# 24 of 50 input-projection tiles as 12 pairs of seven block products each

## Chip, cores and metric

The kernel runs on one core of a Trainium2 chip. The metric is the device time of one execution in microseconds (us); the profile shows one execution of it on that core. Engines are named as in the profile: PE is TensorE, DVE VectorE, ACT ScalarE, POOL GpSimd, SP the SyncE queue.

## What is computed

One layer of a decoder trunk for 2048 prompt tokens and 32 sample tokens (2080 columns in all). One input projection feeds attention (A), an S5 state-space branch with a gated linear unit (B) and a gated linear recurrence (C); each is multiplied by its SiLU gate, projected, merged with sigmoid gates, projected once more and normalized. All in float32.

```python
proj = x @ p['w_in']                                  # 1024 -> 6400 columns
q, k, v, g_a, u_b, g_b, x_c, g_c, g_m = jnp.split(proj, _split_points(), axis=-1)
attn = _attn_prompt(q, k, v, rel_bias, p['sinks'])    # or _attn_sample
y_b, h_re, h_im = _s5_branch(u_b, ...)
y_c, lru_h, conv_new = _rglru_branch(x_c, ...)
ya = (attn * jax.nn.silu(g_a)) @ p['w_br_a']          # yb, yc in the same way
merged = ga * ya + gb * yb + gc * yc                  # ga, gb, gc = sigmoid(g_m)
y = _layernorm(DN_ALPHA * x + merged @ p['w_out'], p['ln_g'], p['ln_b'])
```

## The kernel before

The 6400 projection columns are 50 tiles of 128: u (4 tiles, S5 input), x (4, recurrence input), k, v, q (4), m (24, merge gates), and gc, gb, ga (4 each, the branch gates). A tile is multiplied with five token units `UN` of 512, 512, 512, 272 and 272 columns. `gemm(i, u)` makes one unit: eight steps over the 1024 inputs, each three matmuls (`mm3`, L98 to L101) because every float32 operand is split into a high and a low part: high x high, high x low, low x high. Results lie in a ring of three PSUM banks `mm` and are evacuated by `evac`: u, x, k, v, q and m through `spill` (L187) to DRAM, m after a tanh; a gate tile is multiplied by its branch's result at once (tanh on ACT, two products on DVE, L104 and L229/L233), which `gate_load` has fetched from hD, zD or aD, and is stored to actD by SP (L1403).

Weights of a tile are loaded by SP (`w_load`, L163) into the one buffer `wr` and split into `wh` (ACT) and `wl` (DVE, L94).

The order is written by hand: the instructions of each engine stand in the order in which the program issues them. Between the matmuls of the tiles the program issues side work: `tick` adds up matmul time, and when the pace (`STEP` 4.6, or what a stream asks for) is reached, `side_step` takes the next step of the stream in front: `s5_stream`, then `glu_stream`, `lru_stream`, `attn_stream` and the sample part. The S5 head stores a table `biD` and reads it back as `bsD` (L308, L311), loads its C and D weights (L444, L448) and builds products for which TensorE's first matmul is at L466. The GLU makes two products for each of eight steps, into banks `sa` and `sb`, with `gelu_b` of the next step behind the second (names zs, zy, zh, zl). The recurrence makes 20 products L887 into `sa`, whose results four tanh read (names R, ig), then xf, the convolution of a later chunk and the split f. Attention has 32 steps, two for each of 16 blocks: scores in `sa`, S on DVE, probabilities split into pth and ptl, masks on GpSimd (L1082), products into `sb` (L1100).

After the tiles come the branch products (`py`, L99 to L101, from actD), which begin with the work of `seam`, and the output projection with the normalization (`po`, L1492 to L1494).

Of the kernel before, what the change touches and what calls it, by code (L numbers as in the profile page):

```python
# [16 lines left out]
T = 2080  # L17
# [13 lines left out]
GLU_WEIGHTS = 2.0  # L31
ATT_SCORE, ATT_SOFTMAX = 2.5, 3.5
# [4 lines left out]
         + [("m", i) for i in range(24)]  # L37
         + [("gc", i) for i in range(4)] + [("gb", i) for i in range(4)] + [("ga", i) for i in range(4)])
# [15 lines left out]
def kernel(ctx: ExitStack, tc: tile.TileContext, I, O):  # L54
# [28 lines left out]
    nD = dt_("nD", [2, 32, 128])  # L83
    bsD_t = dt_("bsD", [32, 132])
    bsD = bsD_t[:]
    actD = {b: dt_("actD" + b, [4, 128, T]) for b in "cba"}

# [45 lines left out]
    for u, (t0, n) in enumerate(UN):  # L133
        X[u] = (xhp.tile([128, 8, n], FR, name=f"xh{u}", tag=f"xh{u}"), xlp.tile([128, 8, n], FR, name=f"xl{u}"))
# [25 lines left out]
    def w_load(i):  # L160
        if i < len(TILES):
# [3 lines left out]
    def w_split(i):  # L165
        if i < len(TILES):
            wh = wpool.tile([128, 8, 128], FR, name=uid("wh"), tag="wh")
            wl = wpool.tile([128, 8, 128], FR, name=uid("wl"), tag="wl")
            split(wh, wl, WR.pop(i))
            WS[i] = (wh, wl)  # L170

    def gemm(i, u):
# [4 lines left out]
        for k in range(8):  # L177
            mm3(ps[:, :n], wh[:, k, :], wl[:, k, :], xh[:, k, :], xl[:, k, :], k == 0, k == 7)
            if k < 7:
                tick(n)  # L180
# [11 lines left out]
    def evac(kind, i, u, ps):  # L192
# [21 lines left out]
        elif kind == "m":  # L214
            spill(ps, n, mD[i][:, t0:t0 + n], AF.Tanh, 0.5)
        else:
            b = kind[1]
            gt = gp[0].tile([128, 512], FT, name=uid("gt"), tag="gt", bufs=2)[:, :n]
            br = gate_br.pop((b, i, u))
            act(gt, ps[:, :n], AF.Tanh, scale=0.5)  # L220
            stt(gt, gt, 1.0, ps[:, :n], OP.add, OP.mult)
            st = stage.tile([128, 512], FT, name=uid("st"), tag="st")[:, :n]
            if b == "b":
                nch = min(n, TP - t0) // 8
                V.tensor_mul(st[:, :nch * 8].rearrange("p (c j) -> p c j", j=8),
                             gt[:, :nch * 8].rearrange("p (c j) -> p c j", j=8),
                             br[:, :, 0:nch].rearrange("p j c -> p c j"))
                if u == 4:
                    V.tensor_mul(st[:, 240:272].rearrange("p (b t) -> p b t", t=4),  # L229
                                 gt[:, 240:272].rearrange("p (b t) -> p b t", t=4),  # L230
# [526 lines left out]
    def lru_stream():  # L757
# [123 lines left out]
        for i in range(4):  # L881
# [40 lines left out]
            if i + 1 < 4:  # L922
                yield
# [744 lines left out]
```

## Time and profile before

| | us |
|---|---|
| median of 3 runs | 1797.2 (1795.53 to 1797.56) |
| profiled execution | 1798.88 |
| its span, first to last instruction | 1797.1 |
| PE busy | 1775.0 (99%) |
| DVE busy | 1130.8 (63%) |
| ACT busy | 653.8 (36%) |
| POOL busy | 167.9 (9%) |

PE's busy share is that of the records, whose matmuls overlap a little; the step from one matmul to the next is read from the starts in the timeline. In brackets behind a row of the timeline stands how long the engine was idle before it, and what released it. A row of the waits lists engine and line, what it waited for, the total in us, how many times, and the longest.

### The profile page before, as it was taken

To read this page: it belongs to the slowest core of one execution; us is meant where nothing else is said; L and a number is where in the kernel's file an instruction comes from. 1 tells how busy PE (TensorE), PEld (TensorE's weight loads), DVE (VectorE), ACT (ScalarE), POOL (GpSimd) and SP (SyncE) were. 2 spreads that over 40 slices of the span, in tenths; PEclk is the share of its full clock that TensorE was granted. 3 is DMA by queue.
4 is the path that set the end of the run, shared out by engine and by line. 5 is a ranking of instruction groups with operands and counts; after the bars stand their busy time and mean duration, and the time that the engine had idled before them with its cause. 6 is when DMAs were issued, how large, how long until landed. Compare 5 with 4: busy or idle time off the path is not lost. (4 is left out here: it accounts for less than half of the span.)

```text
span 1797.1 us, 26615 instructions
## 1 busy us (share of the span) xinstructions
PE 1775.0 (99%) x9788; PEld 1549.5 (86%) x9788; DVE 1130.8 (63%) x2450; ACT 653.8 (36%) x1382; POOL 167.9 (9%) x377
## 2 busy tenths in 40 slices
PE   8999999999999999999999999999999999999998
PEld 7888888888899888888988888888888888888886
DVE  5755888886334456653777899654343557666666
ACT  6312443343333287674565655311220202111110
POOL 0000000000000000000355555400000000000000
PEclk9999999999999999999999999999999999999999
DMA  7443333433333334443332334453455646542222
GB/s 235 111 135 100 111 109 112 116 108 92 120 120 114 101 93 123 104 103 95 103 104 85 119 120 134 106 165 101 143 176 155 185 137 189 186 140 94 94 94 77
DMA packets 214038, 220.36 MB, mean 123 GB/s; under 512 B 89125, under 2 KB 156709, under 8 KB 212741
## 3 DMA queue, kind: packets, MB, share of 16 engines
q1 hardware_dynamic: 182532, 169.27, 33.2%
q10 hardware_dynamic: 31376, 49.39, 7.8%
q8 instruction: 77, 1.26, 0.3%
q14 instruction: 53, 0.43, 0.1%
HBM read 136.53 MB, written 83.14 MB: 122 GB/s over the span
## 5 line engine op out<-in xcount | busy, mean ns | idle before, releaser
L99 PE MATMUL mm<-xh,wh 128*128 128x512 f32 (+1 forms) x1920 | 678.9, 354 | 0.0
L101 PE MATMUL mm<-xh,wl 128*128 128x512 f32 (+1 forms) x1920 | 673.5, 351 | 0.0
L100 PE MATMUL mm<-xl,wh 128*128 128x512 f32 (+1 forms) x1920 | 671.4, 350 | 0.0
L101 PEld LDWEIGHTS mm<-xh,wl 128*128 128x128 f32 x1920 | 361.5, 188 | 47.0 <-DVE wl L94 0.3
L99 PEld LDWEIGHTS mm<-xh,wh 128*128 128x128 f32 x1920 | 362.0, 189 | 43.4
L100 PEld LDWEIGHTS mm<-xl,wh 128*128 128x128 f32 x1920 | 362.1, 189 | 42.9
L99 PE MATMUL py<-ah,wbh 128*128 128x512 f32 (+1 forms) x480 | 168.9, 352 | 1.5 <-DVE acc L104 1.5
L101 PE MATMUL py<-ah,wbl 128*128 128x512 f32 (+1 forms) x480 | 168.9, 352 | 0.0
L100 PE MATMUL py<-ah,wbh 128*128 128x512 f32 (+1 forms) x480 | 168.8, 352 | 0.0
L89 ACT ACTIVATE st<-mm 128x512 f32<-128x512 f32 (+1 forms) x170 | 86.9, 511 | 157.2 <-PE mm L101 146.2
L99 PEld LDWEIGHTS py<-ah,wbh 128*128 128x128 f32 x480 | 90.2, 188 | 14.7 <-issue 1.9
L100 PEld LDWEIGHTS py<-ah,wbh 128*128 128x128 f32 x480 | 90.3, 188 | 12.8
L101 PEld LDWEIGHTS py<-ah,wbl 128*128 128x128 f32 x480 | 90.2, 188 | 12.5
L94 DVE TENSOR_TENSOR wl<-wr,wh 128x1024 fp32r<-128x1024 f32 x48 | 58.9, 1226 | 38.1 <-ACT wh L89 38.0
L104 DVE SCALAR_TENSOR_TENSOR gt<-gt,mm 128x512 f32<-128x512 f32 (+1 forms) x60 | 35.0, 584 | 71.1 <-ACT gt L89 70.9
L104 DVE SCALAR_TENSOR_TENSOR br<-br,py 128x512 f32<-128x512 f32 (+1 forms) x80 | 46.9, 586 | 50.9 <-PE py L101 42.5
L89 ACT ACTIVATE gt<-mm 128x512 f32<-128x512 f32 (+1 forms) x60 | 30.9, 515 | 114.4 <-PE mm L101 114.4
L89 ACT ACTIVATE wbh<-wbr 128x512 fp32r<-128x512 f32 x24 | 15.1, 629 | 147.7 <-PE py L100 125.6
L89 ACT ACTIVATE wh<-wr 128x1024 fp32r<-128x1024 f32 x48 | 50.5, 1052 | 23.8 <-DMA wr<-in_w_in_dram 14.5
L104 DVE SCALAR_TENSOR_TENSOR zy<-zs,zy 128x528 f32<-128x528 f32 x16 | 11.3, 709 | 75.4 <-ACT zs L89 75.4
L104 DVE SCALAR_TENSOR_TENSOR acc<-br,py 128x512 f32<-128x512 f32 (+1 forms) x38 | 22.1, 588 | 46.2 <-PE py L101 37.8
L1492 PE MATMUL po<-woh,mg 128*128 128x512 f32 x128 | 49.8, 389 | 0.0
(347 smaller groups left out, 2916.5 us busy)
## 6 DMA issues: line engine op xcount, KB each, us to landing
wr<-in_w_in_dram SPq DMA_DIRECT2D x48, 512.0 KB
mD<-st ACTq DMA_DIRECT2D x72, 256.0 KB
br<-mD SPq DMA_DIRECT2D x71, 256.0 KB
lx<-in_xr_dram SPq DMA_DIRECT2D x16, 512.0 KB
mD<-st ACTq DMA_DIRECT2D x48, 136.0 KB
br<-mD SPq DMA_DIRECT2D x47, 136.0 KB
xr<-in_xT_dram SPq DMA_DIRECT2D x24, 256.0 KB
wbr<-in_w_br_dram SPq DMA_DIRECT2D x24, 256.0 KB
```

The source lines that it names most:

```text
L89: return A.activation(out, in_, func, bias=bias, scale=scale, **kw)
L94: V.tensor_sub(lo, src, hi)
L99: PE.matmul(ps, wh, xh, start=start, stop=False)
L100: PE.matmul(ps, wh, xl, start=False, stop=False)
L101: PE.matmul(ps, wl, xh, start=False, stop=stop)
L104: return (eng or V).scalar_tensor_tensor(out, a, s, b, op0=op0, op1=op1)
L1492: PE.matmul(ps[c], h[:, k, :rows], wh, start=k == 0, stop=False)
```

## The change

The first 26 tiles (u, x, k, v, q, m 16 to 23, m 8 to 11) are made as before. The other 24 (`LATER`: gb, ga, m 12 to 15 and 0 to 7, gc) make only units 2 to 4 in their turn. Their first 1024 tokens, units 0 and 1, are made at the end, in 12 pairs of neighbouring tiles: the two tiles, the two token units and the two halves of the 1024 inputs are 2 x 2 blocks, and seven products of block sums take the place of eight. One product is four steps of three matmuls of 512 columns.

What comes with it:
- `x_sums` makes four sums of blocks of the input on GpSimd right after the second unit of tile 2 and stores them in tD; `x_part` loads and splits them before the pairs.
- The pairs' weights are loaded a second time (`pair_load`), added on GpSimd and split (`operand`); ACT copies a bank out (`keep`), DVE adds a later bank to it, and `finish` makes the tanh or the gate.
- Gates a and b of units 2 to 4 are stored ungated (gD). `gating` loads them and the branch result into two buffers of the ring `gt` (two buffers in all), multiplies on GpSimd and stores to actD: for b inside the attention steps, for a in a new last stream `gating_stream` of 12 steps. Before the first gate pair, gc, all side work that is left is issued.
- All weight loads after the first two tiles go from GpSimd's queue; wl of the `LATER` tiles is made by GpSimd.
- The transposed v of attention uses the bank `sc` instead of a bank `mm`. The paces of GLU, recurrence and sample go from 4.6 to 2.0, 3.4 and 3.0.

```diff
+GLU_WEIGHTS, GLU, LRU = 2.0, 2.0, 3.4
+ATT_SCORE, ATT_SOFTMAX, SAMPLE, SWEEP = 2.5, 3.5, 3.0, 2.0
...
-            WD.dma_start(WR[i], I["w_in"][i])
+            G.dma_start(WR[i], I["w_in"][i])
...
+            (G if o >= FULL else V).tensor_sub(wl, r, wh)
...
+    def gating(b, i, u):
...
+        z = gp[0].tile([128, 512], FT, name=uid("gt"), tag="gt", bufs=2)
+        g = gp[0].tile([128, 512], FT, name=uid("gt"), tag="gt", bufs=2)[:, :n]
...
+            LD.dma_start(z, aD[i][:, t0:t0 + n])
+        LD.dma_start(g, gD[b][i][:, t0:t0 + n])
+        def fin():
...
+                G.tensor_mul(g, g, z)
+            LD.dma_start(actD[b][i][:, t0:t0 + n], g)
...
+    def gating_stream():
+        for i in range(4):
+            for u in range(2, 5):
+                fin = gating("a", i, u)
+                yield SWEEP
+                fin()
...
+    def x_sums():
+        for k in range(4):
+            r11, r12, r21, r22 = (early.tile([128, 512], FT, name=uid("xr"), tag="xr", bufs=6) for _ in range(4))
+            for r, k0, c0 in ((r12, k, 512), (r11, k, 0), (r22, k + 4, 512), (r21, k + 4, 0)):
+                LD.dma_start(r, I["xT"][k0 * 128:k0 * 128 + 128, c0:c0 + 512])
+            G.tensor_sub(r11, r12, r11)
+            G.tensor_sub(r12, r22, r12)
+            G.tensor_sub(r22, r22, r11)
+            G.tensor_sub(r21, r21, r22)
+            for x, r in ((0, r11), (2, r12), (1, r22), (3, r21)):
+                LD.dma_start(tD[x][:, k], r)
...
+        while TILES[p][0] != "m" and sides:
+            side_step()
+        bank, kept = {}, {}
+        for j in range(7):
...
+            into, first = ((0, True), (1, True), (0, False), (2, True), (0, False), (2, False), (3, True))[j]
...
+            for k in range(4):
+                for n, (a, b) in enumerate(((w[:, 0, k], mh[k]), (w[:, 0, k], ml[k]), (w[:, 1, k], mh[k]))):
+                    PE.matmul(ps, a, b, start=first and k == 0 and n == 0, stop=k == 3 and n == 2, skip_group_check=True)
...
+            operand(q + AHEAD)
...
+            if j == 0 and TILES[p][0] != "m":
+                z_load(p, 0)
+                z_load(p + 1, 1)
+            if j == 3:
+                pair_load(p + 4)
+            if j == 0:
+                kept[1] = keep(ps)
+            elif j == 1:
+                V.tensor_add(kept[1], ps, kept[1])
+                finish(p, 0, kept[1])
+            elif j == 2:
+                kept[2] = keep(ps)
```

SP's queue at the S5 head, before (xr is an input unit, wr a tile's weights, p the S5 parameters):

```order
L1254 DMA xr_471<-in_xT_dram 128x272
L1254 DMA xr_475<-in_xT_dram 128x272
L163 DMA wr_564<-in_w_in_dram 128x1024
L163 DMA wr_755<-in_w_in_dram 128x1024
L308 DMA biD<-p_668 8x128x384
L311 DMA bsD<-biD 16x1x132 x2
L163 DMA wr_1098<-in_w_in_dram 128x1024
L444 DMA p_1258<-in_s5c_dram 128x512
L448 DMA p_1262<-in_s5d_dram 128x512
```

and after, the last of the four groups of `x_sums` and what follows it:

```order
L1458 DMA xr_812<-in_xT_dram 128x512
L1458 DMA xr_811<-in_xT_dram 128x512
L1458 DMA xr_814<-in_xT_dram 128x512
L1458 DMA xr_813<-in_xT_dram 128x512
L1464 DMA tD<-xr_811 128x512
L1464 DMA tD<-xr_812 128x512
L1464 DMA tD<-xr_814 128x512
L1464 DMA tD<-xr_813 128x512
L320 DMA biD<-p_673 8x128x384
L323 DMA bsD<-biD 16x1x132 x2
L456 DMA p_1327<-in_s5c_dram 128x512
```

The two weight loads have left the queue, and 16 loads and 16 stores stand ahead of the store to biD.

SP's queue at the first gc work, before (br holds the recurrence's result for a gate; qr, kr and vr belong to attention):

```order
L956 DMA vr_10450<-vD 128x128
L1108 DMA aD<-oo_10482 128x4x128
L1380 DMA br_10661<-hD 128x512
L1380 DMA br_10663<-hD 128x512
L951 DMA qr_10686<-qD 128x4x128
L954 DMA kr_10688<-kD 128x256
L956 DMA vr_10690<-vD 128x128
L1403 DMA actDc<-st_10711 128x512
L1380 DMA br_10714<-hD 128x512
```

and after (gt holds z or the stored gate in turn; the first six rows are the last two of twelve groups of three):

```order
L1269 DMA gt_13089<-aD 128x272
L1270 DMA gt_13090<-gDa 128x272
L1282 DMA actDa<-gt_13090 128x272
L1269 DMA gt_13095<-aD 128x272
L1270 DMA gt_13096<-gDa 128x272
L1282 DMA actDa<-gt_13096 128x272
L1563 DMA gt_13117<-hD 128x512
L1563 DMA gt_13119<-hD 128x512
L1563 DMA gt_13143<-hD 128x512
L1433 DMA actDc<-st_13121 128x512
```

Where a gc load stood between attention's loads, it now stands behind the gating of branch a.

GpSimd's queue in one attention block, before (masks ptq, pth, ptl of two steps, vn the transposed v):

```order
L1082 AFFINE_SELECT pth_9812<-pth_9812 64x256 x2
L1082 AFFINE_SELECT ptl_9813<-ptl_9813 64x256 x2
L991 COPY vn_9870<-vn_9870 64x512
L992 COPY vn_9870<-vn_9870 64x2x256
L993 COPY vn_9870<-vn_9870 64x256
L994 COPY vn_9870<-vn_9870 64x256
L1082 AFFINE_SELECT ptq_9940<-pth_9938 64x256
L1082 AFFINE_SELECT ptq_9940<-ptl_9939 64x256
L1082 AFFINE_SELECT ptq_9940<-pth_9938 64x256
L1082 AFFINE_SELECT ptq_9940<-ptl_9939 64x256
L1082 AFFINE_SELECT pth_9938<-pth_9938 64x256 x2
L1082 AFFINE_SELECT ptl_9939<-ptl_9939 64x256 x2
```

and after:

```order
L1276 TENSOR_TENSOR gt_9571<-gt_9571,gt_9570 128x272
L187 TENSOR_TENSOR wl_9754<-wr_9599,wh_9753 128x1024
L1094 AFFINE_SELECT ptq_9809<-pth_9807 64x256
L1094 AFFINE_SELECT ptq_9809<-ptl_9808 64x256
L1094 AFFINE_SELECT ptq_9809<-pth_9807 64x256
L1094 AFFINE_SELECT ptq_9809<-ptl_9808 64x256
L1094 AFFINE_SELECT pth_9807<-pth_9807 64x256 x2
L1094 AFFINE_SELECT ptl_9808<-ptl_9808 64x256 x2
L178 DMA wr_9834<-in_w_in_dram 128x1024
L1003 COPY vn_9871<-vn_9871 64x512
L1004 COPY vn_9871<-vn_9871 64x2x256
L1005 COPY vn_9871<-vn_9871 64x256
```

Ahead of a step's masks stand now a gating product (gt) and the subtraction for wl, behind them a weight load.

## Rows read from the trace of the kernel before

**Rows 1.** The page: span, busy time of the engines, granted clock in slices.

```profile
span 1797.1 us, 26615 instructions
...
PE 1775.0 (99%) x9788; PEld 1549.5 (86%) x9788; DVE 1130.8 (63%) x2450; ACT 653.8 (36%) x1382; POOL 167.9 (9%) x377
...
PEclk9999999999999999999999999999999999999999
```

**Rows 2.** Waits of PE: line, waited for, total us, times, longest.

```profile
PE mm L99 <- ACT xh L89: 4.8, 1, 4.8
PE sc L1052 <- DVE S L1012: 2.8, 5, 1.1
PE sb L1100 <- POOL ptl L1082: 1.8, 3, 1.2
```

**Rows 3.** Timeline of PE: start us, us, instruction; 512 and 272 columns.

```profile
1449.73 0.39 PE L100 MATMUL py<-ah,wbh 128*128 128x512 f32 x1
...
1451.83 0.39 PE L100 MATMUL py<-ah,wbh 128*128 128x512 f32 x1
...
1452.30 0.29 PE L99 MATMUL py<-ah,wbh 128*128 128x272 f32 x1
...
1453.93 0.28 PE L100 MATMUL py<-ah,wbh 128*128 128x272 f32 x1
```

**Rows 4.** Timeline of DVE at the S5 head.

```profile
64.63 1.21 DVE L94 TENSOR_TENSOR wl<-wr,wh 128x1024 fp32r<-128x1024 f32 x1
...
115.45 0.69 DVE L440 TENSOR_TENSOR p<-p,p 128x512 f32<-128x512 f32 x1
```

**Rows 5.** Timeline of SP's queue at the S5 head.

```profile
66.24 0.33 SPq L308 DMA_DIRECT2D biD<-p  x1
103.70 1.42 SPq L311 DMA_DIRECT2D bsD<-biD  x2
...
105.66 0.42 SPq L444 DMA_DIRECT2D p<-in_s5c_dram  x1
```

**Rows 6.** Groups of POOL: count, busy us, mean ns, idle before.

```profile
L991 POOL CAST vn<-vn 64x512 fp32r<-64x512 f32 x16 | 12.9, 806 | 56.9 <-DMA mD<-st 54.1 <-DVE vn L94 2.0
```

**Rows 7.** Timeline of SP's queue and ACT: loads and first use.

```profile
1318.60 0.80 SPq L1303 DMA_DIRECT2D ar<-actDc  x2
...
1321.64 1.30 ACT L89 ACTIVATE ah<-ar 128x512 fp32r<-128x512 f32 x2 [3.08 <-DMA ar<-actDc]
```

**Rows 8.** Timeline of PE: the S5 head's first product.

```profile
118.12 0.30 PE L466 MATMUL sc<-p,p 128*128 128x32 f32 x2
```

**Rows 9.** Timeline of ACT and DVE behind a GLU product in sb.

```profile
505.91 0.61 ACT L89 ACTIVATE zs<-sb 128x528 f32<-128x528 f32 x1 [3.17 <-PE sb L101]
...
507.18 1.25 DVE L104 SCALAR_TENSOR_TENSOR zy<-zt,zy 128x1056 f32<-128x1056 f32 x1
509.59 1.26 DVE L96 SCALAR_TENSOR_TENSOR zl<-zy,zh 128x1056 fp32r<-128x1056 f32 x1 [1.15 <-ACT zh L89]
```

**Rows 10.** Timeline of PE and ACT in the recurrence.

```profile
639.81 0.62 PE L887 MATMUL sa<-f,lwh 128*128 128x512 f32 x2
...
645.88 0.53 PE L887 MATMUL sa<-f,lwh 128*128 128x284 f32 x2
...
642.12 0.90 ACT L89 ACTIVATE f<-xf 64x284 fp32r<-64x284 f32 x2 [0.46 <-DVE xf L104]
...
645.14 0.68 ACT L89 ACTIVATE ig<-sa,lsm 64x512 f32<-64x512 f32 x1
```

**Rows 11.** Timeline of POOL, DVE and PE in attention.

```profile
1045.20 1.64 POOL L991 CAST vn<-vn 64x512 fp32r<-64x512 f32 x1
...
1045.14 1.22 DVE L94 TENSOR_TENSOR wl<-wr,wh 128x1024 fp32r<-128x1024 f32 x1 [0.72 <-ACT wh L89]
...
1055.58 0.39 PE L1100 MATMUL sb<-ptl,vn 128*128 128x256 f32 x1 [0.32 <-POOL ptl L1082]
```

**Rows 12.** Waits of SP's queue: loads behind a store.

```profile
SPq L688 <- DMA zD<-zy: 15.6, 6, 2.6
```

More of the change, by code (lines that the diff above doesn't have):

```diff
@@ L1289, with raw_tile @@
     ring = [0]
[L1291 removed]
+    def raw_tile(first=False):
         ring[0] += 1
[L1293 to L1294 removed]
         if first or ring[0] % 2:
@@ new lines, in gate_load, with gates_out, gate_next @@
+    def gate_load(ti, u):
+        t0, n = UN[u]
+        br = gp[0].tile([128, 512], FT, name=uid("br"), tag="br", bufs=3)[:, :n]
+        LD.dma_start(br, hD[ti][:, t0:t0 + n])
+        gate_br[(ti, u)] = br
+    def gates_out():
+        while gate_st:
+            LD.dma_start(*gate_st.pop(0))
+    units = [(o, u) for o in range(2, len(TILES)) for u in (range(5) if o < FULL else range(2, 5))]
+    gated = [(ORDER[o], u) for o, u in units if TILES[ORDER[o]][0] == "gc"]
+    def gate_next(iu):
+        if iu in gated:
+            x = gated.index(iu)
+            if x + 1 < len(gated):
+                i, u = gated[x + 1]
+                gate_load(TILES[i][1], u)
@@ L1385, with x_part @@
+    def x_part(x, k, r):
+        if k == 0:
+            if x == 1:
+                t = place("xl2")
+                TT[x] = t[:, 0:4], t[:, 4:8]
+            else:
+                TT[x] = [place(tag) for tag in {2: ("xh1a", "xl1a"), 3: ("xh3", "xh4"), 4: ("xl3", "xl4")}[x]]
+        LD.dma_start(r, tD[x - 1][:, k])
+        split(TT[x][0][:, k], TT[x][1][:, k], r)
+    prev_o = 0
+    for o, u in units:
+        i = ORDER[o]
         kind, ti = TILES[i]
-        if kind == "x" and ti == 0:
+        p = 0 if prev_o != o else p + 1
+        prev_o = o
+        if kind == "x" and ti == 0 and p == 0:
@@ L1390 @@
             hold[0] = 0
-            sides += [glu_stream(), lru_stream(), attn_stream()]
-        if kind == "gc":
+            sides += [glu_stream(), lru_stream(), attn_stream(), gating_stream()]
+        gates_out()
+        if (i, u) == gated[0]:
             while not gp:
                 side_step()
-        if kind == "ga":
-            while not prompt_done[0]:
-                side_step()
-        if kind[0] == "g" and ti == 0:
-            gate_load(kind[1], ti, 0)
-        order = UORD if i == len(TILES) - 1 else list(range(5))
@@ L1420 @@
-    while gate_st:
-        LD.dma_start(*gate_st.pop(0))
+            gate_load(ti, u)
+        gate_next((i, u))
+        ps = gemm(i, u)
+        if p == 0:
+            w_split(o + 1)
+        if p == 1:
+            w_load(o + 2)
+        evac(kind, ti, u, ps)
+        if o == 2 and p == 1:
+            x_sums()
+        if FULL <= o < FULL + 4 and p == 1:
+            x_part(2, o - FULL, stage.tile([128, 512], FT, name=uid("st"), tag="st"))
+        hold[0] = int(a_done[0] and kind == "u")
```

355 lines of the change are left out of this document (235 added, 120 removed).

## Prediction

> **What bounds the kernel now.** The page's busy table comes first: TensorE is busy 1775.0 of 1797.1 us at full granted clock [rows 1]. The table of waits agrees: no entry of TensorE is above 4.8 us, the largest two inside the run of the tiles are 2.8 and 1.8 us, both in attention [rows 2]. So one matmul less is worth its start spacing, as long as every chain on the other engines keeps ending before TensorE asks for it. The spacing is in the timeline: nine steps from 1449.73 to 1451.83 us are 0.233 us for 512 columns; 13 steps from 1452.30 to 1453.93 are 0.125 us for 272 [rows 3]. What has to be found in this change is which chains now end late: it takes TensorE time away and moves or shortens the cover that the side work had.
>
> **The gain.** 12 pairs take 7 products of 4 x 3 matmuls of 512 columns, 84, where two tiles took 2 x 2 x 24 = 96: 144 fewer, x 0.233 = **33.5 us** less. All other matmuls keep count and shape.
>
> **S5 head (x_sums).** SP's queue now holds 16 loads and 16 stores of x_sums ahead of the biD store, and the first of those stores waits for GpSimd's first subtraction, which stands behind the weight load of tile 4 in GpSimd's queue, and that waits for the wl subtraction that ends at 64.63 + 1.21 = 65.84 us [rows 4]. Before, biD left at 66.24 and bsD, which waits for it to land, at 103.70, 37.5 us later; the s5c load at 105.66 [rows 5]. GpSimd's two-input 128x512 is not in the trace: from below VectorE's 0.69 us for that shape [rows 4], from above 1.6, twice the 0.806 of GpSimd's 64x512 copy [rows 6] (one pass for each input); I take 1.2, the middle. The first four end at 67 + 4.8 = 72. Six buffers hold four tiles of a group, so each later group waits for loads that stand behind the stores of the one before: 3.5 us (a load takes 3.0 from issue to use, 1318.60 to 1321.64 [rows 7], with its issue behind the others) + 4.8, three times: biD leaves at 97, bsD's wait ends at 134.5, and s5c leaves at 136; with 2.7 to land, 1.0 for the small steps and 4.2 for the six VectorE operations (the last ended at 116.14 [rows 4]) TensorE's first product of the head starts at 144 instead of 118.12 [rows 8]. Nothing stands ahead of it that could be done meanwhile: TensorE's order up to there is unchanged. Cost **26 us** (18 with 0.69, 33 with 1.6).
>
> By the Trainium skill ("GPSIMD Engine Reference", Elementwise — side-by-side cycle accounting) a two-input operation on GpSimd takes 1.96 times VectorE's time; with VectorE's row that would be an estimated 1.35 us, and the head would cost 28 us instead of 26. No run here shows it.
>
> **GLU.** Its pace falls from 4.6 to 2.0, so fewer matmuls stand between two products. After a product in bank sb comes a fixed chain: zs on ScalarE from 505.91, two VectorE steps to 508.43, zh on ScalarE, zl from 509.59 to 510.85 [rows 9], and the next product in sa needs zl. That is 5.0 us from the end of sb. Before, TensorE had 5.3 to 5.6 us of matmuls there; by its order now 12 to 18, between 2.2 and 2.85 us, 18.5 us in seven gaps. 7 x 5.0 - 18.5 = **17 us** (14 to 19: a gap's end is known to 0.4 us).
>
> **LRU.** Each step's product reads what the step before made, and its bank is free when four tanh have read it. The chain is the one before: the products start 6.07 us apart (639.81, 645.88), and the last tanh ends at 645.14 + 0.68 = 645.82 [rows 10]; between them ig leads to xf, that to the conv steps, these to f (ends 643.02) and this to four tanh, one behind the other, with no gap that the shorter pace would take out: 6.17 us with what lies around it. Offered now are 3.97 to 4.19 us of matmuls and 0.93 or 0.52 of product: 5.12, 4.9, 5.06 and 4.71. Against 6.17, and 5.3 for the last one with 284 columns, that is 4.0 us per i, x 4 = **16 us** (6 if the ScalarE evictions in the chain step aside, 22 if the 512-column steps, whose conv is longer, decide).
>
> **Attention.** GpSimd gets the gating product (every other step), the wl subtraction of 128x1024 and the weight issue on top of selects and copies that already make TensorE wait for ptl (0.32 us at 1055.58 [rows 11]). Its 167.9 us [rows 1] lie nearly all in the 16 blocks, some 10 us a block, of some 18 us by TensorE's order; about 5 come in. Each lands behind a select or ahead of one; a wl on GpSimd stands behind the selects of a step, while TensorE now has only two units of 272 columns (6.0 us) before it wants it. One row shows contention besides: a copy that means 0.806 took 1.64 us at 1045.20, beside VectorE's wl [rows 6, 11]. In the other direction VectorE loses the wl and gate work that stood ahead of S. I take 0.4 us for each of 26 steps, **10 us** (-5, if the relief of VectorE removes the 5 us of waits [rows 2], to 30, all of 26 steps with 1.2).
>
> **Start of the pairs.** Weights and sums for the first pair go into tiles that the last units of 272 columns free only 6.0 us before its start; load 3.0, split 1.3, behind GpSimd's queue: **6 us** (3 to 12).
>
> **The gating of branch a.** Twelve steps (load z, load g, GpSimd product, store) share a ring of two buffers, z in one and g in the other, so the next g waits until the last store has landed. The last nine steps are issued in one burst just before the first gc pair, and the third waits for the sample's output store; the loads of the gc pair stand behind them on SP. A step of 512 columns is 1.2 product, 2.6 for the store (loads that waited for a store to land: 15.6 us in 6 [rows 12]) and 3.04 for a load: 6.84; of 272 columns 0.65 + 2.6 + 3.04 = 6.3. Three and six of them are 58.3; the third step, from the sample's end, 6.3; the gc load 3.0: z is there 67.6 us after the sample's last product. By its order TensorE has 39 matmuls left of the pair before (9.1 us) and then products j = 0 to 3 of the gc pair (48 matmuls, 11.2); j = 4 adds into a bank that ScalarE has to copy out first, and ScalarE stands behind a tanh that waits for VectorE's product with z. 67.6 - 20.3 = **47 us** (34 with steps 1.4 shorter, 56 with 1 us more each).
>
> **Hidden.** The pairs themselves: 84 x 0.233 = 19.6 us of TensorE against some 9 of ScalarE, 13 of VectorE and four GpSimd operations. If the GpSimd operations took 3 us each they would still fit. Weight loads leave SP; nothing on the path waited for them. The branch outputs and the output projection stay.
>
> **Sum.** -33.5 + 26 + 17 + 16 + 10 + 6 + 47 = +88.5 us: span 1885.6, profiled execution 1887.4 (1798.88 before, 1.8 around the span), and, since the median of the runs stood 1.7 below the profiled one, a median of **1886 us**.
>
> **Rivals.** (a) *Not slower: the chains were paced by TensorE.* I read each chain's length from a trace in which TensorE set the rhythm. If its parts close up once TensorE asks sooner, places GLU, LRU, head and drain alike, only the start of the pairs is left: 1797.2 - 33.5 + 3 = 1767. For it: in the GLU rows the first wait ends on TensorE [rows 9]. Against it: inside the chains the releasers are ScalarE, VectorE and DMA, and the drain is DMA landing. It decides from where the stalls add up to less than 33.5 us of my 122. Chance 0.13, and 0.03 for about equal.
> (b) *The drain does not reach TensorE.* If the nine steps run at the pace of the loads alone, 3.0 each, 27 + 9 - 20 = 16 us instead of 47: 1855; without any stall 1839. For it: SP is idle. Against it: two buffers. Chance 0.14.
> (c) *GpSimd and VectorE exclude each other.* Should every GpSimd two-input operation wait out a VectorE one (1.64 against 0.806 at 1045.20 [rows 6, 11]), 16 x 0.8 = 13 us come to the head and 20 to attention: 1919. Against it: the sixteen copies of that shape mean 0.806 with the slow one among them. Chance 0.13.
>
> The Trainium skill ("SBUF — State Buffer", SBUF: two separate sides) states that VectorE and GpSimd share a port pair by an exclusive lock, when VectorE reads two SBUF inputs and GpSimd reads SBUF; that is rival (c). The one slow copy agrees; it is a single row.
>
> **How the numbers follow.** Forecast 0.57, (b) 0.14, (c) 0.13, (a) 0.16 with the equal part. About 0.2% (3.6 us) is what a measurement of this kernel can tell from no change. The range leaves out (a) and little more: from 1832, where (b) meets short stalls elsewhere, to 1930, which takes in (c) and the upper bounds of head and drain. Faster 0.13, same 0.03, slower 0.84.
>
> **What the next profile would show.** Right: TensorE idle about 26 us ahead of its line of the head's kernel products with SP in x_sums before; seven idles of 2 to 3 us in the GLU, released by zl; 16 of about 1 us in the LRU released by ig; one of over 30 us in the first gc pair, released through ScalarE by a load of z. Wrong: GpSimd subtractions under 0.7 us, biD leaving before 80 us, gating steps under 4 us, or a first gc pair without a gap. The forecast falls if head and drain together cost less than 20 us.

## The result and the profile after

The median of four runs is 2061.85 us (2060.03 to 2063.6) beside 1796.37 us (1793.81 to 1797.56) of the kernel before on the same chip: 1.148 times, 95% interval 1.146 to 1.150. The forecast was 1886 us, its range ended at 1930. The direction was right, a third of the size was seen.

The page of the kernel after, lines answering to [rows 1]:

```profile
span 2060.1 us, 27166 instructions
...
PE 1808.0 (88%) x9644; PEld 1561.5 (76%) x9644; DVE 1280.7 (62%) x2546; ACT 735.4 (36%) x1530; POOL 365.5 (18%) x565
...
PEclk9979999999999998889999997986999999999999
```

9788 - 9644 is the 144 matmuls that were to go. At before's clock TensorE would be busy 1775.0 - 33.5 = 1741.5 us; it is busy 1808.0, which is **66.5 us** more. The bracketed idles of TensorE's rows add up to 243.6 us, where they were 13.7: **229.9 us** more. 229.9 + 66.5 - 33.5 = 262.9 is the whole difference of the spans (2060.1 - 1797.1 = 263.0).

Most of the 66.5 us is the clock. The dips of PEclk lie where the idles lie, and in the stretches with a granted clock of 0.50 TensorE was busy for 112.8 us (6.8 before). Half of that is what the lower clock took: 56.4 - 3.4 = **53.0 us** more than before. The other 13.5 us belong to the idles themselves: the records overlap (0.39 us each against a step of 0.233), so at each of the 71 further breaks in TensorE's work the last record counts in full. That part is an estimate, about 0.2 us a break.

The waits of TensorE after, answering to [rows 2] (line, waited for, total us, times, longest):

```profile
PE mm L1616 <- ACT br L96: 58.5, 4, 53.8
PE sc L1064 <- DVE S L1024: 40.2, 15, 5.2
PE sa L899 <- ACT ig L96: 37.9, 11, 14.7
PE mm L106 <- DVE st L111: 19.9, 4, 8.4
```

From above: the drain of gating a (the wait for its last steps ahead of the first gate pair; 53.8 is one wait), attention, the recurrence, again the recurrence (the gate tiles issued beside it). Summed by stage from the rows (us of idle):

| | start | head | GLU | LRU | attention | pairs | tail | sum |
|---|---|---|---|---|---|---|---|---|
| before | 4.8 | 0 | 0 | 0 | 7.4 | – | 1.5 | 13.7 |
| after | 4.8 | 31.6 | 14.5 | 58.7 | 45.4 | 86.8 | 1.9 | 243.6 |

**Head.** SP's queue after, answering to [rows 5] (start us, issue us):

```profile
67.88 4.50 SPq L1464 DMA_DIRECT2D tD<-xr  x4
...
78.65 4.61 SPq L1464 DMA_DIRECT2D tD<-xr  x4
...
106.11 0.30 SPq L320 DMA_DIRECT2D biD<-p  x1
143.88 1.45 SPq L323 DMA_DIRECT2D bsD<-biD  x2
145.38 0.44 SPq L456 DMA_DIRECT2D p<-in_s5c_dram  x1
```

Groups of x_sums follow each other every 11 us, biD leaves at 106.11 (97 in the forecast) and lands 37.8 us later. TensorE's rows there, answering to [rows 8], and ahead of them a weight load on GpSimd's queue with the split that waits for it:

```profile
108.03 0.57 POOL L178 DMA_DIRECT2D wr<-in_w_in_dram  x1
132.33 1.06 ACT L96 ACTIVATE wh<-wr 128x1024 fp32r<-128x1024 f32 x1 [23.92 <-DMA wr<-in_w_in_dram]
```

```profile
133.93 0.60 PE L106 MATMUL mm<-xh,wh 128*128 128x272 f32 x1 [15.73 <-ACT st L96]
134.32 0.43 PE L107 MATMUL mm<-xl,wh 128*128 128x272 f32 x1
134.55 0.43 PE L108 MATMUL mm<-xh,wl 128*128 128x272 f32 x1
...
138.11 0.29 PE L106 MATMUL mm<-xh,wh 128*128 128x272 f32 x1
138.23 0.29 PE L107 MATMUL mm<-xl,wh 128*128 128x272 f32 x1
...
152.22 0.60 PE L478 MATMUL sc<-p,p 128*128 128x32 f32 x2 [12.45 <-DVE p L449]
```

The head's first product starts at 152.22 instead of 118.12. The longer of the two idles ahead of it, 15.73 us, doesn't end on biD: the weight load stands in GpSimd's queue behind the subtractions, ScalarE stands 23.92 us for it, and the evictions that TensorE needs stand behind ScalarE's split. The second, 12.45 us, ends on p, at the end of biD's chain, and sets when the head starts; the first lies inside the same delay.

The same rows show the clock: behind an idle of 15.73 us the step of 272 columns is 0.23 us (134.32 to 134.55), at a granted clock of 0.50, which is 1.2 GHz; then it is 0.12 again (138.11 to 138.23), at 1.00, which is 2.4 GHz.

**Recurrence.** One place holds the two longest waits. ScalarE, then SP's queue, then TensorE:

```profile
819.56 0.63 ACT L96 ACTIVATE T<-st 128x512 fp32r<-128x512 f32 x1 [16.20 <-DMA st<-tD]
```

```profile
812.41 0.39 SPq L844 DMA_DIRECT2D out_conv_s_dram<-lx  x1
812.85 0.57 SPq L1473 DMA_DIRECT2D st<-tD  x1
```

```profile
824.49 1.22 PE L899 MATMUL sa<-f,lwh 128*128 128x512 f32 x2 [14.69 <-ACT ig L96]
```

`x_part(2)` loads a sum and splits it in the same step. The load stands on SP behind copies of the recurrence that wait for DMA, so it leaves 9.5 us after ScalarE came to the split (803.36), and ScalarE stands, with the recurrence's tanh behind it.

**Attention.** Groups of VectorE after, in the form of [rows 6] (count | busy us, mean ns | idle before):

```profile
L111 DVE SCALAR_TENSOR_TENSOR q<-qr,q 64x256 fp32r<-64x256 f32 x64 | 66.5, 1078 | 1.0
L111 DVE SCALAR_TENSOR_TENSOR xf<-xf,R 128x2104 f32<-128x2104 f32 x4 | 13.5, 3387 | 0.1
```

Before, the two means were 531 and 2351 ns for the same shapes. VectorE became slower at work that the change doesn't touch, and not evenly. The first group with its shortest, median and longest time in ns, then one place of GpSimd and VectorE:

```profile
L111 DVE SCALAR_TENSOR_TENSOR q<-qr,q x64: 411/518/5578, 894.7 to 1233.0; 64x256 fp32r<-64x256 f32 x64
```

```profile
938.01 1.56 POOL L1276 TENSOR_TENSOR gt<-gt,gt 128x512 f32<-128x512 f32 x1
939.54 2.33 POOL L187 TENSOR_TENSOR wl<-wr,wh 128x1024 fp32r<-128x1024 f32 x1
936.14 6.02 DVE L111 SCALAR_TENSOR_TENSOR q<-qr,q 64x256 fp32r<-64x256 f32 x2
```

The median is what it was before (517 ns, the longest then 626); 13 of the 64 rows take 1.2 to 5.6 us. Here VectorE's pair of steps ends at 942.16, 0.3 us after GpSimd's gating product and wl are both through.

**Drain.** The last product of the sample part, the first product of gating a, a later step of it on SP, and VectorE's product for the first gc gate; then TensorE's rows at the gate pairs:

```profile
1350.62 1.97 PE L1248 MATMUL sc<-PN,vnn 4*128 4x32 f32 x16
1362.86 1.29 POOL L1281 TENSOR_TENSOR gt<-gt,gt 128x512 f32<-128x512 f32 x1
1412.35 0.32 SPq L1282 DMA_DIRECT2D actDa<-gt  x1
1412.77 0.38 SPq L1269 DMA_DIRECT2D gt<-aD  x1
1414.37 0.32 SPq L1270 DMA_DIRECT2D gt<-gDa  x1
1425.50 0.69 DVE L1575 TENSOR_TENSOR gt<-st,gt 128x512 f32<-128x512 f32 x1 [56.07 <-DMA gt<-hD]
```

```profile
1427.91 4.76 PE L1616 MATMUL mm<-T,ws 128*128 128x512 f32 x12 [53.77 <-ACT br L96]
...
1463.65 5.78 PE L1616 MATMUL mm<-T,ws 128*128 128x512 f32 x24 [0.70 <-ACT st L96]
...
1552.38 8.45 PE L1616 MATMUL mm<-T,ws 128*128 128x512 f32 x36 [0.67 <-ACT st L96]
```

From store to store, steps of 512 columns take 5.9 to 6.0 us and steps of 272 some 4.9 (5.8 the first). GpSimd's first gating product stands behind the pairs' additions on its queue and ends 11.6 us after the sample's last product (1352.59); eleven more steps take 58.0 us, and the gc load 3.4. Of these 72.9 us TensorE had work for 21.6.

Behind the drain, four pairs take 1552.38 - 1463.65 = 88.7 us, 22.2 each; the eight blocks of a pair, 96 matmuls at 0.233, are 22.4. Among them the saved product is given back to waits for evacuations (0.6 to 2.7 us, two in some pairs).

### The profile page after: what moved, and what is told of

It is laid out like the page before. It is cut to its first block, busy times and chain, and to the rows that moved or that the text cites. A ratio compares the mean times of both kernels' runs of the same rounds, so it can differ in the third digit from the quotient of the medians.

```text
span 2060.1 us, 27166 instructions
## 1 busy us (share of the span) xinstructions
PE 1808.0 (88%) x9644; PEld 1561.5 (76%) x9644; DVE 1280.7 (62%) x2546; ACT 735.4 (36%) x1530; POOL 365.5 (18%) x565
## 4 chain that ended last, share of the span: by engine, by line
PE 56%; DVE 18%; DMA 10%; ACT 8%; issue 5%; POOL 2%; SPq 1%; ACTq 0%; DVEq 0%; POOLq 0%
PE mm L106 8%; PE mm L108 8%; PE mm L107 8%; PE mm L1616 4%; PE py L106 4%; PE py L108 4%; PE py L107 4%; PE po L1723 3%; PE po L1721 3%; PE po L1722 3%; DVE q L111 3%; DMA biD<-p 2%; DVE xf L111 2%; DVE gt L1575 1%; ACT R L96 1%
## 5 line engine op out<-in xcount | busy, mean ns | idle before, releaser
L106 PE MATMUL mm<-xh,wh 128*128 128x272 f32 (+1 forms) x1344 | 464.5, 346 | 35.6 <-DVE st L111 19.9
L108 PE MATMUL mm<-xh,wl 128*128 128x272 f32 (+1 forms) x1344 | 457.9, 341 | 4.3 <-POOL wl L187 2.4
L107 PE MATMUL mm<-xl,wh 128*128 128x272 f32 (+1 forms) x1344 | 456.9, 340 | 0.0
L106 PEld LDWEIGHTS mm<-xh,wh 128*128 128x128 f32 x1344 | 263.9, 196 | 59.2 <-DVE st L111 20.8
L108 PEld LDWEIGHTS mm<-xh,wl 128*128 128x128 f32 x1344 | 261.8, 195 | 30.3 <-POOL wl L187 2.8
L107 PEld LDWEIGHTS mm<-xl,wh 128*128 128x128 f32 x1344 | 262.8, 196 | 22.0
L1616 PE MATMUL mm<-T,ws 128*128 128x512 f32 x576 | 147.6, 412 | 71.4 <-ACT br L96 58.5
L1616 PEld LDWEIGHTS mm<-T,ws 128*128 128x128 f32 x576 | 112.9, 199 | 101.9 <-ACT br L96 60.9
L107 PEld LDWEIGHTS py<-ah,wbh 128*128 128x128 f32 x480 | 90.3, 188 | 12.8
L108 PEld LDWEIGHTS py<-ah,wbl 128*128 128x128 f32 x480 | 90.2, 188 | 12.5
L101 DVE TENSOR_TENSOR ws<-wraw,ws 128x512 fp32r<-128x512 f32 x72 | 55.7, 777 | 44.1 <-ACT ws L96 44.1
L1616 PE MATMUL mm<-xh,ws 128*128 128x512 f32 x192 | 62.9, 396 | 7.6 <-ACT ws L96 7.3
L111 DVE SCALAR_TENSOR_TENSOR q<-qr,q 64x256 fp32r<-64x256 f32 x64 | 66.5, 1078 | 1.0
```

The costliest lines, as they stand in the source:

```text
L101: V.tensor_sub(lo, src, hi)
L106: PE.matmul(ps, wh, xh, start=start, stop=False)
L107: PE.matmul(ps, wh, xl, start=False, stop=False)
L108: PE.matmul(ps, wl, xh, start=False, stop=stop)
L111: return (eng or V).scalar_tensor_tensor(out, a, s, b, op0=op0, op1=op1)
L1616: PE.matmul(ps, a, b, start=first and k == 0 and n == 0, stop=k == 3 and n == 2, skip_group_check=True)
```

## Experiments

Each run is one time beside one time of the kernel before (1795.8 to 1801.4 us), so a few us between two of them mean nothing; the idles by stage carry the verdicts. The expectations name theories by letters and say themselves what each means there: in most, A is that the idle of a stage hangs on the wait or order that the edit takes away, B that something else ends last, C that GpSimd and VectorE hinder each other; T and W are those of the last three runs. The diffs are against the kernel after, except where the text says before.

### The paces alone, on the kernel before

```diff
+GLU_WEIGHTS, GLU, LRU = 2.0, 2.0, 3.4
...
-            yield
+            yield GLU
...
-                yield
+                yield LRU
```

> The kernel before (1797 us) with nothing but the shorter paces of GLU (2.0) and recurrence (3.4). Theory A: the chains of GLU and recurrence are as long as they were, so TensorE idles seven times some 2 us in the GLU (14.5 us in the changed kernel) and some 26 us in the recurrence (what the changed kernel shows there without the waits for x_part), and the granted clock drops behind it: 1835 to 1860. Theory B (the side work ends earlier, and time is given back later): 1790 to 1810.

1840.96 us beside 1801.4: the shorter paces cost **39.6 us** by themselves. Idle: GLU 14.5, recurrence 21.6, attention 1.1 (7.4 before); busy 12.8 more. Waits of TensorE in this run:

```profile
PE sa L887 <- ACT ig L89: 17.2, 12, 4.8
PE sa L99 <- ACT zh L89: 8.2, 7, 1.6
PE sa L100 <- DVE zl L96: 6.3, 7, 0.9
```

The seven waits each for zh and zl are those of the kernel after (8.2 and 6.3 us there too), behind the chain of [rows 9]. So the chains are fixed lengths and don't close up when TensorE asks sooner. In the recurrence, 13.6 of the 21.6 us are three waits of 4.4 to 4.8 us at the second product of a new channel tile; the other ten waits take 0.5 to 2.2 us each.

### x_part's loads a unit ahead, from ScalarE's queue

```diff
+        if FULL <= o < FULL + 4 and p == 0:
+            PX.append(stage.tile([128, 512], FT, name=uid("st"), tag="st"))
+            ST.dma_start(PX[0], tD[1][:, o - FULL])
...
-            x_part(2, o - FULL, stage.tile([128, 512], FT, name=uid("st"), tag="st"))
+            split(TT[2][0][:, o - FULL], TT[2][1][:, o - FULL], PX.pop(0))
```

> The changed kernel with the four loads of x_part(2) issued from ScalarE's queue one unit ahead of their split, instead of from SP's queue right in front of it. Theory A: ScalarE stood 16.2 and 8.1 us at the split T<-st waiting for a load that was stuck on SP behind the recurrence; the idles of TensorE between 800 and 893 us (14.7, 1.3, 7.3, 8.4, 4.8, together 36 us) fall below 12, span 2060 - 24 to - 40, 2020 to 2036. Theory C (they come from VectorE and GpSimd getting in each other's way, the wl subtraction of 3.6 us at 788 us among them): the idles there stay over 25 us and the span over 2045.

2024.34 us; recurrence idle 58.7 → 31.6, the other stages within 2 us. Waits of TensorE in this run:

```profile
PE sa L899 <- ACT ig L96: 19.6, 11, 4.7
...
PE mm L106 <- DVE st L111: 11.2, 3, 5.3
```

The waits of up to 14.7 us are gone. What is left is the 21.6 us of the paces and some 10 more. These answer to the 11.2 us on `st` from VectorE, which the paces alone don't show: gate tiles now stand beside the recurrence, and their evacuation stands on VectorE behind xf and the convolution. That last part is read from the waits, not tried.

### wl on GpSimd alone, on the kernel before

```diff
-            split(wh, wl, WR.pop(i))
+            r = WR.pop(i)
+            act(wh, r, AF.Copy)
+            (G if i >= 26 else V).tensor_sub(wl, r, wh)
```

> The kernel before with nothing but the wl subtraction of tiles 26 to 49 on GpSimd (about 2.5 us each there, 1.2 on VectorE). Theory C (a two-input operation on GpSimd holds VectorE's off): VectorE's operations in attention take longer, q<-qr,q or S<-S by over a fifth in the mean, TensorE's waits rise by 5 to 25 us, 1800 to 1825. Theory D (only GpSimd's queue matters): VectorE's means stay within 5% and the time within 5 us of 1797.

1813.91 us beside 1801.4, **12.5 us** slower for 24 subtractions moved off the fuller engine. Attention idles 20.0 us (7.4 before). Groups of VectorE in this run:

```profile
L104 DVE SCALAR_TENSOR_TENSOR q<-qr,q 64x256 fp32r<-64x256 f32 x64 | 41.7, 690 | 11.6 <-ACT q L89 10.5
...
L1044 DVE TENSOR_TENSOR S<-S 128x256 f32<-128x256 f32 x32 | 21.8, 681 | 1.1
```

531 and 440 ns before. One group alone lengthens the means of VectorE's steps by 30 and 55%; again the medians stay (516 and 425 ns), and single rows take up to 4.1 us.

### wl and the gating products on VectorE, in the kernel after

```diff
-            (G if o >= FULL else V).tensor_sub(wl, r, wh)
+            V.tensor_sub(wl, r, wh)
...
-                G.tensor_mul(g, g, z)
+                V.tensor_mul(g, g, z)
```

> The changed kernel with the wl subtraction of the later tiles and the gating products on VectorE instead of GpSimd. Theory C (two-input work on GpSimd holds VectorE up): VectorE's q<-qr,q of 64x256 falls from 1078 ns back to about 530, kl<-kr,k from 709 to about 510, TensorE's waits for S fall from 40 us to under 10, attention's clock rises, span 1985 to 2015. Theory D (it is only GpSimd's queue that is late, VectorE's longer times have another cause): q<-qr,q stays near 1.0 us; VectorE gets 24 x 1.2 us more work and the span is over 2040.

2010.58 us; attention idle 45.4 → 17.4, though VectorE has more to do. A group of VectorE and a wait of TensorE in this run:

```profile
L111 DVE SCALAR_TENSOR_TENSOR q<-qr,q 64x256 fp32r<-64x256 f32 x64 | 33.1, 556 | 1.0
```

```profile
PE sc L1064 <- DVE S L1024: 11.1, 9, 5.9
```

q is back at 556 ns from 1078, with no row over 633, and xf at 2350. TensorE's waits for S on VectorE fall from 40.2 to 11.1 us; its waits for GpSimd's masks were 3.3 us in the kernel after and are not what fell. With the run before it this shows rival (c) in attention: while GpSimd does two-input work on SBUF, VectorE's own two-input work is held. The Trainium skill ("SBUF — State Buffer", SBUF: two separate sides) calls it an exclusive lock on a shared port pair; the trace agrees (1078 against 556 ns).

### The sums left out of the head

```diff
-        if o == 2 and p == 1:
-            x_sums()
...
-        LD.dma_start(r, tD[x - 1][:, k])
+        LD.dma_start(r, I["xT"][k * 128:k * 128 + 128, 0:512])
```

> The changed kernel without x_sums: no loads, sums or stores for them, and x_part loads plain blocks of the input in place of the sums (the loads keep shape and count; this part of the computation is left out). Theory T, the sums' transfers near biD's store cost the head: biD leaves near 66 us and lands some 37 us later, the head's idle falls from 31.6 to under 5 us, and with the clock that comes back (the runs so far gave 1.3 to 1.4 us for each us of idle) the time is 2018 to 2032 us. Rival W, weight loads from GpSimd's queue or another moved wait cost the head: idle stays above 20 us and the time above 2045 us.

This run leaves the sums out of the computation; the loads in front of the pairs fetch plain blocks in their place. 2018.82 us, head idle 31.6 → 0. SP's queue in this run, then TensorE at the first product:

```profile
64.46 0.31 SPq L320 DMA_DIRECT2D biD<-p  x1
102.55 1.42 SPq L323 DMA_DIRECT2D bsD<-biD  x2
```

```profile
117.86 0.30 PE L478 MATMUL sc<-p,p 128*128 128x32 f32 x2
```

117.86 is the place of [rows 8]. The head's idle is x_sums and nothing else; the weight loads on GpSimd's queue cost nothing there as long as no subtractions stand ahead of them. 32.2 us of idle brought 43.0 us back; the rest is clock (TensorE at 0.50 for 91.9 us busy instead of 112.8, half of the difference is 10.5).

### The same sums in the GLU phase

```diff
+        xs = x_sums(p)
+        next(xs)
         for j in range(8):
             glu_mm(j, 0)
+            next(xs, None)
...
+            r11, r12, r21, r22 = (p.tile([128, 256], FT, name=uid("xs"), tag="xs", bufs=4) for _ in range(4))
```

> The same sums, complete, made in the GLU phase in eight groups of 256 columns. By T the head's idle falls under 5 us as without the sums, and the GLU's 14.5 us of idle grow by 0 to 8 us, since GpSimd's 32 short subtractions run beside VectorE's part of the GLU chain: 2020 to 2040 us. By W the head stays above 20 us and the time is above 2050 us.

2025.27 us: head 0, GLU 14.5 → 19.8 idle. The repair keeps all of the work and costs 5 us where it now lies.

### The sums behind bsD, spread, and on ScalarE's queue

Three earlier tries kept the sums near biD. The first puts them where the early phase ends:

```diff
+            x_sums()
             ees.close()
...
-        if o == 2 and p == 1:
-            x_sums()
```

> The changed kernel (2062 us) with x_sums issued after the S5 head instead of right after the second unit of tile 2. Theory A (each stall is made locally, the stalls add up, and the lower granted clock follows each of them): the idles of TensorE at the head (1.9, 15.7, 12.5 and 1.2 us at 100 to 154 us) go, the granted clock there rises from 0.87 to over 0.95, and the span falls by 31 to 46 us, to 2015 to 2031. Theory B (what is taken away comes back at the next wait, because the side work as a whole is too long): the head's idles go but the later ones grow, and the span stays within 10 us of 2060.

2070.18 us, head idle 44.4, of which 43.2 is one wait for p. biD lands in time (bsD leaves at 102.20), but the four groups of sums now stand between it and s5c, which leaves at 154.97 instead of 105.66 [rows 5].

The second issues one group per unit on SP:

```diff
+            yield
...
+        if (o, p) in ((2, 1), (2, 2), (2, 3), (2, 4), (3, 0)):
+            next(xs, None)
```

> The changed kernel with the four groups of x_sums spread over five units (loads and subtractions of a group behind one unit, its stores behind the next), so that SP never waits for a subtraction with the biD store behind it. The run with x_sums after the S5 head's first phase showed what counts: SP's place of the 32 transfers against biD and the s5c load; there they stood between bsD and s5c and the head's idle grew to 43 us. Theory A: biD leaves before 75 us, the head's idles (31 us) fall below 8, span 2060 - 23 to - 45, 2015 to 2037. Theory B (GpSimd's subtractions, 1.3 to 1.5 us each, are what the head waits for): biD leaves early, but TensorE still waits over 20 us for p, span over 2045.

2050.38 us, head idle 28.3. Three groups stand between bsD (101.16) and s5c (137.99), but that is not what TensorE waits for: 26.7 us are one wait for ScalarE's eviction us, and that stands behind a memset on GpSimd's queue:

```profile
135.55 0.28 ACT L96 ACTIVATE us<-mm 128x32 f32<-128x32 f32 x2 [36.82 <-POOL us L215]
```

The memset comes behind 12 subtractions, and the first of these waits 37.5 us for loads that stand on SP behind bsD. The third gives the spread groups' DMAs to ScalarE's queue:

```diff
-                LD.dma_start(r, I["xT"][k0 * 128:k0 * 128 + 128, c0:c0 + 512])
+                ST.dma_start(r, I["xT"][k0 * 128:k0 * 128 + 128, c0:c0 + 512])
...
-                LD.dma_start(tD[x][:, k], r)
+                ST.dma_start(tD[x][:, k], r)
```

> The changed kernel with x_sums spread over five units as in the run before, and its 32 transfers issued from ScalarE's queue. That run had left x_sums between bsD and the s5c load on SP, where SP stands 36 us for biD, and the head's idle had stayed at 28 us. Theory A (only SP's place counts): s5c leaves before 108 us, the head's idles (31 us) fall below 10, span 2060 - 21 to - 45, 2015 to 2039. Theory B (16 subtractions of 1.3 us and the weight loads behind them on GpSimd's queue are late too): TensorE waits over 20 us all the same, now for weights or for p.

2057.73 us, head idle 34.8. TensorE's wait, one row of ScalarE, and SP's waits in this run:

```profile
PE mm L106 <- ACT us L96: 34.8, 4, 22.6
```

```profile
103.04 0.40 ACT L96 ACTIVATE us<-mm 128x272 f32<-128x272 f32 x1 [30.81 <-DMA tD<-xr]
```

```profile
SPq L323 <- DMA biD<-p: 35.9, 1, 35.9
SPq L323 <- DMA tD<-xr: 32.5, 2, 31.6
```

All of the idle ends on ScalarE's evictions: ScalarE stands in its own queue at the sums' stores. biD lands as before (35.9 us waited); bsD then waits another 31.6 us, by the profile for a store of the sums, and TensorE has no wait for p in this run. All three missed, each for another reason: behind bsD the sums delay the load of s5c, spread over the units they hold GpSimd's queue, and on ScalarE's queue they hold ScalarE. The theory of the prediction (order on SP ahead of biD) was one of several ways in which the same work, on whatever queue, held something that TensorE needs.

### Gating a early, with a ring of eight, and with loads ahead

The first issues eight of the twelve steps inside the sample part:

```diff
-        for i in range(4):
-            for u in range(2, 5):
+        for u in (2, 3, 4):
+            for i in range(4):
...
-        yield SAMPLE
+        yield sweep()
```

> The changed kernel with the eight gating steps of branch a that need no sample tokens issued between the steps of the sample part, so that four are left for the burst ahead of the first gc pair. Theory A (the burst is one chain of landings through two buffers): the idle of 53.8 us in the first gc pair falls to 5 to 15 us, span 2060 - 39 to - 60 with the clock behind it, 2000 to 2021. Theory B: the waits move into the sample part, whose loads stand behind on SP, and the span stays over 2045.

2038.33 us: the drain's wait falls from 53.8 to 10.9, but a new one of 20.2 us stands at 1335.88, where the pairs' operand additions stand on GpSimd behind gating products that wait for their loads. About half of the gain moved. The second only enlarges the ring:

```diff
-        z = gp[0].tile([128, 512], FT, name=uid("gt"), tag="gt", bufs=2)
+        gt = (lambda: gr[0].tile([128, 512], FT, name=uid("ga"), tag="ga", bufs=8)) if b == "a" else \
```

> The changed kernel with eight buffers of its own for the twelve gating steps of branch a instead of the ring of two. Theory A (the burst is a chain of store, landing and load through two buffers): the idle of 53.8 us in the first gc pair falls to under 15, span 2060 - 39 to - 55, 2005 to 2021. Theory E (it is the number of transfers and of GpSimd products, at 1.3 us each, that takes the time): the idle stays over 30 us.

2046.08 us, drain 53.8 → 44.1. With free buffers the steps are still 4.0 to 5.2 us from store to store, and SP shows why:

```profile
1362.98 0.32 SPq L1284 DMA_DIRECT2D actDa<-ga  x1
1363.39 0.38 SPq L1271 DMA_DIRECT2D ga<-aD  x1
```

SP's queue is in order: a step's loads stand behind the store of the step before, which waits for its product. The third changes that too:

```diff
+                if len(fins) == 4:
+                    fins.pop(0)()
+                fins.append(gating("a", i, u))
                 yield SWEEP
-                fin()
```

> The changed kernel with eight buffers for the gating of branch a and the loads of four steps issued ahead of the first store. With eight buffers alone the idle had only gone from 53.8 to 44.1 us: SP, in order, kept each load behind the store of the step before, a step took 4.0 to 4.6 us (load 3.3 to 4, product 0.8 to 1.3). Theory A (order on SP, not buffers or traffic): a step takes 2 to 2.5 us, the idle in the first gc pair falls below 20 us, span 2060 - 34 to - 55, 2005 to 2026. Theory E (traffic and GpSimd's products): idle over 35 us.

2016.0 us, drain 16.2. So of 53.8 us two buffers account for 9.7, the order of loads and stores for 27.9, and 16.2 remain.

### The repairs together

First e2's loads, wl and gate b's product on VectorE, the ring with loads ahead, and the sums on ScalarE's queue:

```diff
+            V.tensor_sub(wl, r, wh)
...
+                V.tensor_mul(gv, gv, z[:, :, 0:nch].rearrange("p j c -> p c j"))
...
+            ST.dma_start(PX[0], tD[1][:, o - FULL])
...
+                fins.append(gating("a", i, u))
```

> All four repairs together in the changed kernel: x_sums from ScalarE's queue, the x_part loads ahead, wl and branch b's gating product on VectorE, the loads of the last gating ahead. Theory A (local stalls, they add up, the clock follows): idle of TensorE 245 - 31 - 36 - 45 - 40 = about 90 us, its excess of busy time from the low clock (66 us) down to 20 to 35: 1840 to 1885. Theory B (given back elsewhere): over 1910.

1949.72 us, in the range of B and 65 us above that of A. 158.4 us of idle stay where A had some 90: the head was not repaired (35.0), and the repairs of recurrence, attention and drain returned 27, 28 and 38 us, as each did alone, not 36, 45 and 40. Recurrence 32.0, attention 17.2, drain 16.2: the single repairs add up, which is what A says, only to less. Then also the m pairs first and the old pace:

```diff
+         + [("m", i) for i in range(8)] + [(g, i) for g in ("gc", "gb", "ga") for i in range(4)])
...
-            yield GLU
+            yield STEP
...
-            yield LRU
+            yield STEP
```

> The four repairs, and besides the six m pairs ahead of the gate pairs and the pace back to 4.6 behind a GLU product in sb and at the end of a recurrence chunk, where the kernel before with the short paces alone had stood 14.6 and some 19 us (it took 1841 where the kernel before took 1797). Theory A: those idles go as well, the drain has 39 us more of cover: 1790 to 1835. Theory B: the side work, 42 us later by TensorE's order, runs into the gate pairs and the time stays over 1850.

1944.29 us, again in the range of B. GLU 0.8 and recurrence 24.0, but with the longer paces attention reaches into the first pairs, whose idle is 67.7 instead of 52.2. The cover was only moved. Last, the same with the sums in the GLU phase:

```diff
-        if o == 2 and p == 1:
-            x_sums()
...
+        xs = x_sums(p)
+        next(xs)
```

> All repairs together: the sums in the GLU phase, x_part's loads a unit ahead, wl and gate b's product on VectorE, the ring of eight for gating a with loads four steps ahead, the m pairs first and pace 4.6 in GLU and recurrence. The run with all but the first of these took 1944.3 us with 34 us idle in the head. By T 30 us of idle go, and some clock: 1900 to 1915 us. By W 1935 to 1945 us. Both say slower than before: some 110 us of idle stay, of which two thirds lie among the pairs.

1913.16 us beside 1795.79: 125.3 us of idle less than the kernel after, 148.7 us of time. 118.3 us of idle stay, 69.0 of them among the pairs. TensorE's two largest waits in this run are 21.5 us for ScalarE's br, 15.8 of it behind gating a, and 18.8 us for attention's S, whose last steps now lie among the pairs.

No version tried beats the kernel before.

## Why the prediction failed

| term | forecast | idle measured | shown by |
|---|---|---|---|
| gain, 144 matmuls | -33.5 | -33.5, worked out | count on the page |
| S5 head | 26 | 31.6 | sums left out: 0 |
| GLU | 17 | 14.5 | paces alone: 14.5 |
| recurrence | 16 | 58.7 | paces alone 21.6, x_part's loads 27.1, some 10 left open |
| attention | 10 | 38.0 more than before | GpSimd's products 28.0 |
| start of the pairs | 6 | 7.3 | wait for ws |
| drain of gating a | 47 | 53.8 | ring and order 37.6 |
| pairs otherwise | 0 | 25.7 | waits, not taken apart; 7.9 of it in attention steps among the pairs |
| clock | 0 | 53.0 of the 66.5 of busy time | busy time at a granted clock of 0.50 |

**Right.** The places and most mechanisms. The GLU's seven gaps, the start of the pairs and the drain came within 7 us each, and the paces' part of the recurrence (21.6) at the end of its range. In the recurrence that is partly luck: the forecast had 16 waits of about 1 us between products, and there were ten with 8.0 us together; 13.6 us came from three places that it had not seen. In the head the GpSimd subtraction was nearly right (1.27 to 1.36 us on 15 of 16 rows against 1.2), but the loads of a group took 4.9 us to first use instead of 3.5, so a group took 11 us where I had 8.3. The first product came 34 us later, my upper bound was 33. The forecast gave the weight loads no cost; one of them held ScalarE for 23.92 us, though without moving the head's start.

The drain's size fits better than its working. Its steps were shorter (5.9 to 6.0 and 4.9 us against 6.84 and 6.3), but two more of them than forecast came behind the sample's end, and the first product stood behind the pairs' additions on GpSimd: 72.9 us to z where the forecast had 67.6, with 21.6 us of cover against 20.3. Two buffers made 9.7 us of it, the order of loads and stores on SP 27.9.

**Step that failed, first: the clock.** The sum added idles and took TensorE's work at full clock throughout. The runs show that idles cost a second time: the busy time beyond that of the kernel before was 66.5 us for 243.6 of idle after, 42.9 for 118.3 with all repairs, 12.8 for 43.2 with the paces alone. Of these the lower granted clock took 53.0, 30.3 and 8.7 us. It was the largest missing term. The kernel before had little to show of it: 13.7 us of idle and two short dips of the clock, which cost it 3.4 us and don't appear in the digits of its page.

**Second: the recurrence.** The forecast followed the DMAs of x_sums and not those of x_part. Its load and split in the same step made ScalarE wait for SP's queue (16.20 us on one row); taking that wait away returned 27.1 us of idle.

**Third: attention.** I priced it at 0.4 us a step and left rival (c) at 0.13, because sixteen copies meant 0.806 us with one slow row among them [rows 6]. That reading of the mean was wrong: by their single rows three of the sixteen took 1.63 to 1.64 us, each beside VectorE's two-input wl, as the one in [rows 11], and thirteen took 0.61 to 0.70. The slow rows were the evidence, and the mean hid them. The rival was right here: 28.0 us of idle, where it had 20 on top of 10. It was wrong for the head, where one subtraction of sixteen was slow (2.25 us).

**Fourth: the pairs were costed at nothing.** The busy sums of the other engines fit, but the order did not: products that add to a bank wait for its evacuation, and ScalarE and VectorE have `finish` in between. Behind the drain a pair took 22.2 us instead of 19.6, against 22.4 for what it replaced. That `finish` is the reason is read from the waits and the order; no run tried it.

**The rivals (a) and (b).** (a) fell with the paces alone: the chains are as long when TensorE asks sooner. (b) fell with the drain's 53.8 us; its figure of 16 us was reached only with eight buffers and loads ahead of stores (16.2), and there by chance, at some 1.9 us a step instead of its 3.0.

The range failed for the same reason: it added the bounds of the terms that I had and left no room for the clock, which belongs to all of them.

## What to carry to other kernels

When a change makes a fully busy TensorE idle, add to the idles what the clock takes behind them; here TensorE's busy time grew by 0.2 to 0.4 us for each us of idle in the kernels with over 40 us of it (46.0 for 212.8 to 42.9 for 118.3), and of these the lower granted clock took 0.14 to 0.26 us (30.5 and 30.3). Follow each moved load to the engine that waits for it in order, and ask what stands ahead of it on its queue, and what then stands behind it: a transfer moved to a compute engine's queue holds that engine's other work. Two-input work moved to GpSimd "because it is free" is paid by VectorE, so look at the neighbours afterwards and not only at the moved instructions, and at their longest rows besides their means.

## What the runs showed of the hardware

- VectorE's 64x256 two-input step went from 531 to 1078 ns in the mean, and a 128x2104 one from 2351 to 3387, with GpSimd's products beside them; the median of the first stayed (517 and 518 ns), and single rows took up to 5.6 us. Single-input reductions did not move (686 ns before and after), and neither did attention's additions of a PSUM and an SBUF operand (at most 958 ns before and after).
- GpSimd took 1.27 to 1.36 us for a 128x512 two-input operation and 2.49 in the mean for 128x1024, where VectorE's are 0.69 and 1.22.
- The biD store, 1.5 MB in pieces of 384 numbers, took 36 to 38 us to land, also beside 32 transfers issued from ScalarE's queue (35.9 us waited); what those transfers held was ScalarE, for 30.81 us.
- Behind an idle of 15.73 us the matmuls from 133.93 to 137.7 ran at 1.2 GHz (granted clock 0.50), those from 138.11 at 2.4; in the stretch from 240 to 480 us, where TensorE had no idle, the granted clock was 1.00 throughout.
